# Where the operands of a seven-product round are split, in a one-core decoder step in float32

## The chip, the cores and the metric

The kernel runs on one core of a Trainium2 chip. It has a matrix engine (PE), three elementwise engines (DVE, the VectorE; ACT, the ScalarE; POOL, the GpSimd) and a queue (SP) from which nearly all DMA transfers of this kernel are issued, in the order in which they stand in the program. The metric is the time of one execution in microseconds. The kernel before takes 2215.38 us as the median of three runs (2211.3 to 2217.26).

## The reference

One layer of a decoder for 1024 prompt tokens and 8 single-token requests, width 1024, all in float32. The tokens are put side by side, T = 1032 columns. What matters here are the two feed-forward steps around the mixer:

```
def swiglu(x, w_up, w_down):
    gate, up = jnp.split(x @ w_up, 2, axis=-1)
    return (jax.nn.silu(gate) * up) @ w_down

hp = layer_norm(ALPHA * hp + 0.5 * swiglu(hp, ffn1_w_up[l], ffn1_w_down[l]), ln1_g[l], ln1_b[l])
...                                   # attention and retention, merged
hp = layer_norm(ALPHA * hp + 0.5 * swiglu(hp, ffn2_w_up[l], ffn2_w_down[l]), ln3_g[l], ln3_b[l])
```

The hidden width is 2816, 22 tiles of 128 features. The mixer between the two steps isn't touched by the change.

## The kernel before, in words

**Numbers in two parts.** A float32 operand is held as a high part, rounded to the matrix engine's fast type fp32r, and a low part, the rest. A product takes three matmuls: high by high, high by low, low by high. To split means: ACT copies x into the high part, and then another engine computes x minus the high part. Weight halves (128x512) are split so as they arrive: `w_hi` on ACT, `w_lo` on DVE.

**Seven products for eight.** Most of the two feed-forward steps is computed by a Strassen-Winograd form of 2x2 blocks. The weights of such a block are a quad of four halves and sums of them (`st`, made by DVE); the other operands are sums of token halves of 516 columns. One product is a unit of 24 matmuls of 258 columns. In the up-projection (units P, seven of them per feature tile, and C for the first tile) the operands are sums of the input. They lie in seven tiles TT[0] to TT[6], each 4T wide: 2T columns of high part, 2T of low part. `t_stage(i)` (L806) makes operand i from the residual tiles `ya` and `yb`: for a sum, two subtractions on DVE, then two ACT copies and two DVE subtractions for the two parts.

**The hidden values.** When a feature tile is done, `hidden` (L1435) gets it as `m`, two token halves. The first two and the last four tiles are stored plainly (`adr`). The sixteen between go in pairs: a is the even tile of a pair, b the odd one. From a pair the seven operands of the down-projection are made and stored to DRAM (`tdr`) as float32 numbers in one part: operand 0 is the first half of a, operand 1 the first half of b, 5 the second half of b, and 2, 3, 4 and 6 are differences (four DVE subtractions of 128x516, into the tiles `s`). There are two rounds (quads) of four pairs in each of the two feed-forward steps, so four rounds in all.

**The down-projection.** Its products are the units S: i = 0 to 6, for n = 0 to 3 in each round. The operands come back into the same seven tiles. As soon as a tile has had its last product (`rested`), `fetch_after` (L944) lets go the read of the next operand into it, at least 2 us of planned PE time after the read before. `fetch_one` (L929) reads 1032 KB from `tdr` into the low part's place, and `split` (L913) then makes the parts in two pieces of 128x1032: ACT copies, and DVE subtracts for operands 0, 2, 4 and 6, POOL for 1, 3 and 5. There are two lanes: the splits of one lane go one after the other, those of DVE and POOL side by side. A round of the down-projection begins with eight short units `dn` of 12 matmuls, which take a plain feature pair (two reads of 516 KB, split in pieces of 128x516, always on DVE). So a round is read while the units before it run: the last seven P units, or the last seven S units of the round before (n = 3), and the eight dn units behind them.

**The order of the work.** The kernel is written out by a planner in Python. It keeps a clock of PE (`E.pe`) and of each engine, a DMA queue (`E.dma` adds a transfer at 0.38 MB per us and 2 us for landing), and emits the side work when its due time comes. Each engine runs its instructions in the order in which they were emitted, whatever the true times are. `split` sleeps until the planned landing plus 1.5 us, and puts a piece on DVE only while DVE's planned backlog is at most 1.3 us (SHORT). `features` (L965) is called ahead of each S unit and finishes by force what its operand still lacks. PE's results are taken out of PSUM by ACT and DVE (`evac`); a PSUM bank is used again one or two units later, so a late evacuation stops PE.

**The tiles of the first step.** In the first feed-forward step the tiles 0 to 3 come from one pool and 4 to 6 from another; the down-projection used them in the order 1, 4, 5, 2, 3, 6, 0 (`qslot`), so its operands were read in the order 0, 3, 4, 1, 2, 5, in which the P units let the tiles go. In the second step the order is 1 to 6, 0.

**The start of the second up-projection.** Its units go C0, C1, P0, P1, C2, C3, P3, P2, then product 0 of the next feature tile, then P4, P5, P6. `before` (L1617) calls `t_stage(4)` ahead of P3 and `t_stage(6)` ahead of P2. The results of P3, P2 and of the next tile's product 0 are taken out by ACT copies.

Of the kernel before, what the change touches and what calls it, by code (L numbers as in the profile page):

```python
# [18 lines left out]
P = 128  # L19
# [17 lines left out]
QUADS = [(1, 2), (3, 4)]  # L37
QJ = [(2, 3, 0, 1), (0, 1, 2, 3)]
ORDER = [0, 1] + [GROUPS[g][k] for q in QUADS for k in range(4) for g in q] + GROUPS[5]
PLAIN = GROUPS[0] + GROUPS[5]  # L40
LAT = 0.2
HT = T // 2
# [6 lines left out]
NWARM = 3  # L49
START = 6.0  # L50
FETCH = 2.0
SHORT = 1.3
POOLD = (1, 4, 6)
AHEAD = 0.5
# [172 lines left out]
def build(tc, I, O):  # L227
# [3 lines left out]
    with ctx:  # L231
# [39 lines left out]
        scs = dram.tile([32, P], F32, name="scs")  # L271
        scv = dram.tile([1, 8, P], F32, name="scv")
        adr = [[dram.tile([P, T], F32, name=f"adr{p}_{i}") for i in range(len(PLAIN))] for p in range(2)]
        tdr = [[[dram.tile([P, 4, HT], F32, name=f"tdr{p}_{q}_{i}") for i in range(7)] for q in range(2)] for p in range(2)]
        hres = dram.tile([P, 4, T], F32, name="hres")
        dq = nc.gpsimd.dma_start
        ds = nc.sync.dma_start
# [24 lines left out]
                sbanks.put(b, E.pe)  # L302

        ta = ctx_open("ta", R)
        TT = [ta.tile([P, 4 * T], F32R, name=f"T{i}") for i in range(4)] + [None] * 3
        env["h"] = TT[:4]
        env["yb"] = ctx_open("y47", L).tile([P, 4, T], F32, name="yb")

        def open_y():
# [7 lines left out]

        def open_tb():
            p = ctx_open("tb", R)
            for i in range(4, 7):  # L320
                TT[i] = p.tile([P, 4 * T], F32R, name=f"T{i}")

        def open_sa():
            p = ctx_open("sw", R)
# [571 lines left out]

        qslot = [[[1, 4, 5, 2, 3, 6, 0], [4, 5, 2, 3, 6, 0, 1]], [[1, 2, 3, 4, 5, 6, 0], [2, 3, 4, 5, 6, 0, 1]]]
        fetches, fstate, rested, splits, lane = [], dict(t=0.0), {}, {}, [None, None]  # L900

        def fill(p):

            s0, s1 = qslot[p]
            res = [(0, ("U", 0), 0, k) for k in range(2)]
            res += [(s, ("U", s), "Q0", s0.index(s)) for s in range(1, 7)]
            res.append((0, "dn0", "Q0", 6))
            res += [(s0[0], (0, 0), 1, k) for k in range(2)]
            res += [(s0[i], (0, i), "Q1", i - 1) for i in range(1, 7)]
            res.append((s0[0], "dn1", "Q1", 6))  # L910
            return res + [(s1[i], (1, i), 5, 2 * i + k) for i in range(2) for k in range(2)]

        def split(hi, lo, n, t, pool):  # L913

            last, lane[pool] = lane[pool], None
            me = lane[pool] = [False]
            yield t
            while last is not None and not last[0]:
                yield E.pe + 0.2
            g = n // 2  # L920
            for k in (0, g):
                while not pool and E.eng["dve"] > E.pe + SHORT:
                    yield E.pe + 0.2
                t = E.act(hi[:, k:k + g], f(lo)[:, k:k + g], n=g)
                yield t
                (E.ptt if pool else E.tt)(lo[:, k:k + g], f(lo)[:, k:k + g], f(hi)[:, k:k + g], ALU.subtract, n=g)
            me[0] = True

        def fetch_one():  # L929
            p, i, _, g, k = fetches.pop(0)  # L930
            x = TT[i]
            if g in (0, 1, 5):
                o = k % 2 * 2 * T
                hi, lo = x[:, o:o + T], x[:, o + T:o + 2 * T]
                ds(out=f(lo), in_=adr[p][k + (2 if g == 5 else 0)])
                n = T
            else:
                hi, lo = x[:, 0:2 * T], x[:, 2 * T:4 * T]
                ds(out=f(lo), in_=tdr[p][int(g[1])][k].rearrange("p k n -> p (k n)"))
                n = 2 * T  # L940
            fstate["t"] = E.pe
            splits.setdefault((i, g), []).append(E.spawn(split(hi, lo, n, E.dma(n * 0.000512) + 1.5, n > T and k % 2)))

        def fetch_after(u):  # L944

            p = u["p"]
            if u["kind"] == "P":
                if u["ft"] != NF - 1:
                    return
                if u["i"] == 0:  # L950
                    fetches.extend((p,) + x for x in fill(p))
                    rested.clear()
                    splits.clear()
                rested["U", u["i"]] = True
            elif u["kind"] == "S" and u["n"] == 3:
                rested[u["q"], u["i"]] = True
            elif u["kind"] == "dn" and u["n"] == 7:
                rested[f"dn{u['part']}"] = True
            while fetches and fetches[0][2] in rested and (E.pe > fstate["t"] + FETCH or fetches[0][4] % 2 and fetches[0][3] in (0, 1, 5)):
                fetch_one()  # L960

        def dn_slot(u):
            return qslot[u["p"]][0][0] if u["part"] else 0

        def features(p, i, g):  # L965

# [468 lines left out]
        def hidden(p, ft, t):  # L1435
# [6 lines left out]
            q, k = (ft - 2) // 8, (ft - 2) % 8 // 2  # L1442
            s = env["s"]

            def out(i, src):
                ds(out=tdr[p][q][i][:, k, :], in_=src)
                E.dma(0.264)

            def sub(i, o, x, y):
                t = E.tt(o, x, y, ALU.subtract, n=HT)  # L1450
                E.later(t, lambda: out(i, o))

            if ft % 2 == 0:
                E.later(t, lambda: out(0, a[0]))
                E.later(t, lambda: sub(3, s[0], a[1], a[0]))
            else:
                E.later(t, lambda: out(1, b[0]))
                E.later(t, lambda: out(5, b[1]))
                E.later(t, lambda: sub(2, s[2], b[1], s[0]))
                E.later(t + 0.7, lambda: sub(4, s[1], b[1], a[1]))  # L1460
                E.later(t + 1.4, lambda: sub(6, s[3], b[0], s[2]))

        def evac_s(j, i, bank):

# [152 lines left out]
        def before(ui, u):  # L1617
            kind, c = u["kind"], u["c"]
            if kind == "P":
                p, ft, i = u["p"], u["ft"], u["i"]  # L1620
                if ft == 1:
# [13 lines left out]
                        stages([], [1] if p else [1, 2, 3])  # L1635
                    elif i == 3:
                        stages([4], [2, 3, 4, 5]) if p else stages([6], [6, 7])
                    elif i == 2 and p:
                        stages([6], [])
                    elif i == 4:  # L1640
                        end_t(p)
                        if p:
                            need(o + 6)
                        env["busy"] = False
# [46 lines left out]
                    start_d(u["p"])  # L1691
                features(u["p"], dn_slot(u), u["part"])
            if kind == "S":
                features(u["p"], qslot[u["p"]][u["q"]][u["i"]], f"Q{u['q']}")
            x = units[ui + 1] if ui + 1 < len(units) else u
            if x["kind"] == "S" and kind == "S" and x["q"] == u["q"]:
                features(u["p"], qslot[u["p"]][x["q"]][x["i"]], f"Q{x['q']}")
            if kind == "down":
                if u["first"]:
                    end_quads(u["p"])  # L1700
                for i in range(2):
                    features(u["p"], qslot[u["p"]][1][i], 5)
            if kind == "k":
                if c == 0:
                    ctx_close("tb")
# [9 lines left out]
        def operands(u):  # L1715
            kind, c = u["kind"], u["c"]
            n0, N = CH[c]
            if kind == "down":
                ks = []
                for i in range(4):  # L1720
                    x = TT[qslot[u["p"]][1][i // 2]]
                    o = i % 2 * 2 * T + n0
                    ks.append((u["dd"] * 4 + i, x[:, o:o + N], x[:, o + T:o + T + N]))
            elif kind in ("ao", "ro"):
# [13 lines left out]
        def product(u, bank):  # L1738

            if u["kind"] in ("P", "S"):  # L1740
                xs = [TT[u["i"] if u["kind"] == "P" else qslot[u["p"]][u["q"]][u["i"]]]]
# [222 lines left out]
```

## Time and profile before

| | |
|---|---|
| runs | 2211.3, 2215.38, 2217.26 us |
| the profiled execution's own time | 2217.32 us |
| its span, first to last instruction | 2215.5 us |
| mean granted PE clock | 0.987 |
| PE busy | 2133.7 us (96%), 15865 matmuls |
| DVE busy | 1495.8 us (68%) |
| ACT busy | 832.6 us (38%) |
| POOL busy | 268.5 us (12%) |
| DMA moved | 233.93 MB |

All times in the trace are us from the span's start. A row of a group gives the line, the engine, the operation, out<-in by tile names, partitions x elements, the count, the busy time, the mean in ns, and then the engine's idle time before these instructions with what ended it. All elementwise instructions are issued by a few helpers, so most have the same line (L119 for DVE, L115 for ACT, L135 for POOL), and the tile names tell them apart: `T<-T` is the split of a down-projection operand that was read from DRAM, `T<-ya` a split in `t_stage`, `yb<-pr` or `ya<-pr` an evacuation.

### The profile page before, as it was taken

What the parts mean: (1) busy time and instruction counts of PE and PEld (TensorE: products, weight loads), DVE (VectorE), ACT (ScalarE), POOL (GpSimd) and SP (SyncE); (2) the same over time, 40 slices, a digit from 0 to 9 for tenths busy, and PEclk for the clock granted to TensorE, in tenths of its full rate; (3) what the DMA queues carried; (4) which work ended last, traced back from release to release, by engine and by line L of the source; (5) the groups of instructions that cost most, each with busy time, mean ns of one, the idle gap of its engine ahead of it and who ended that gap; (6) DMA issues with size and microseconds to landing.
All of it is one profiled execution on the core that took longest, in us unless ns stands there. A gap on an engine that the chain in (4) does not pass through costs nothing.

```text
span 2215.5 us, 39506 instructions
## 1 busy us (share of the span) xinstructions
PE 2133.7 (96%) x15865; PEld 2096.7 (95%) x15865; DVE 1495.8 (68%) x2659; ACT 832.6 (38%) x1569; POOL 268.5 (12%) x259
## 2 busy tenths in 40 slices
PE   8999999999899999999999999998999999999996
PEld 7999999999899889999979999988999999999996
DVE  7666666685856885566676757777666666686757
ACT  5333333342423674111324434553333333433223
POOL 1000000020304333111110202010000000021103
PEclk9999999999999999999999999998999999999998
DMA  4322322261430110111263434531332232444222
GB/s 139 108 89 99 107 95 87 96 252 64 187 120 29 57 51 26 43 40 40 76 194 132 139 124 134 186 116 48 101 101 101 96 106 92 159 167 173 77 96 77
DMA packets 111705, 233.93 MB, mean 106 GB/s; under 512 B 13730, under 2 KB 17666, under 8 KB 107666
## 3 DMA queue, kind: packets, MB, share of 16 engines
q1 hardware_dynamic: 111170, 231.36, 30.9%
q8 instruction: 125, 2.05, 0.4%
q14 instruction: 58, 0.48, 0.1%
q0 software_dynamic: 352, 0.05, 0.0%
HBM read 186.56 MB, written 45.84 MB: 105 GB/s over the span
## 4 chain that ended last, share of the span: by engine, by line
PE 81%; DVE 10%; DMA 3%; issue 2%; ACT 2%; POOL 1%; SPq 0%; DVEq 0%; POOLq 0%; ACTq 0%
PE pr L97 54%; PE mb L97 25%; DVE T L119 2%; DMA raw<-in_w_dram 2%; DVE w_lo L119 2%; DVE ya L119 2%; PE sb L97 1%; DVE yb L119 1%; DVE ln L119 1%; DVE zt L119 1%; PE sb L105 1%; ACT w_hi L115 1%; ACT T L115 0%; POOL pt L135 0%; POOL ln L135 0%
## 5 line engine op out<-in xcount | busy, mean ns | idle before, releaser
L97 PE MATMUL pr<-T,w_hi 128*128 128x258 f32 x7008 | 1145.6, 286 | 45.9 <-DVE ya L119 14.6
L97 PEld LDWEIGHTS pr<-T,w_hi 128*128 128x128 f32 x7008 | 978.3, 192 | 53.0 <-DVE ya L119 14.0
L97 PE MATMUL pr<-T,w_lo 128*128 128x258 f32 x3504 | 713.2, 285 | 0.4 <-DVE w_lo L119 0.4
L97 PEld LDWEIGHTS pr<-T,w_lo 128*128 128x128 f32 x3504 | 551.4, 192 | 0.6 <-DVE w_lo L119 0.6
L97 PE MATMUL mb<-T,w_hi 128*128 128x384 f32 (+1 forms) x2208 | 526.2, 325 | 1.8 <-DVE yb L119 1.8
L119 DVE TENSOR_TENSOR w_lo<-raw,w_hi 128x512 fp32r<-128x512 f32 x500 | 360.0, 738 | 142.3 <-ACT w_hi L115 139.5
L115 ACT ACTIVATE w_hi<-raw 128x512 fp32r<-128x512 f32 x500 | 305.2, 625 | 290.3 <-PE pr L97 186.3
L97 PEld LDWEIGHTS mb<-T,w_hi 128*128 128x128 f32 x2208 | 378.0, 189 | 8.5 <-issue 5.0
L97 PE MATMUL mb<-T,w_lo 128*128 128x384 f32 (+1 forms) x1104 | 353.6, 320 | 0.0
L97 PEld LDWEIGHTS mb<-T,w_lo 128*128 128x128 f32 x1104 | 207.8, 188 | 0.0
L135 POOL TENSOR_TENSOR T<-T 128x1032 fp32r<-128x1032 f32 x24 | 67.1, 2813 | 1010.5 <-ACT T L115 1008.8
L115 ACT ACTIVATE w_hi<-st 128x512 fp32r<-128x512 f32 x174 | 108.4, 630 | 184.8 <-DVE st L119 98.4
L119 DVE TENSOR_TENSOR w_lo<-st,w_hi 128x512 fp32r<-128x512 f32 x174 | 123.1, 726 | 5.7 <-ACT w_hi L115 5.7
L119 DVE TENSOR_TENSOR a<-pr,a 128x516 f32<-128x516 f32 x87 | 60.5, 695 | 98.1 <-PE pr L97 94.4
L115 ACT ACTIVATE a<-pr 128x516 f32<-128x516 f32 x86 | 51.7, 601 | 132.7 <-PE pr L97 132.7
L119 DVE SCALAR_TENSOR_TENSOR ya<-pr,ya 128x516 f32<-128x516 f32 x72 | 49.4, 691 | 56.5 <-PE pr L97 56.3
L119 DVE SCALAR_TENSOR_TENSOR yb<-pr,yb 128x516 f32<-128x516 f32 x72 | 49.3, 691 | 55.5 <-PE pr L97 55.5
L119 DVE TENSOR_TENSOR T<-T 128x516 fp32r<-128x516 f32 (+1 forms) x64 | 86.7, 1354 | 0.0
L115 ACT ACTIVATE T<-T 128x1032 fp32r<-128x1032 f32 (+1 forms) x88 | 74.3, 895 | 15.1 <-DMA T<-tdr 14.4
L115 ACT ACTIVATE th<-a 128x516 f32<-128x516 f32 x43 | 27.3, 635 | 124.3 <-DVE a L119 124.3
L119 DVE TENSOR_TENSOR ln<-pr,ln 128x516 f32<-128x516 f32 x43 | 29.9, 695 | 53.5 <-PE pr L97 53.5
L119 DVE SCALAR_TENSOR_TENSOR gt<-gt,mb 128x384 f32<-128x384 f32 (+1 forms) x48 | 24.4, 509 | 59.8 <-PE mb L97 58.2
(316 smaller groups left out, 2230.2 us busy)
## 6 DMA issues: line engine op xcount, KB each, us to landing
raw<-in_w_dram SPq DMA_DIRECT2D x500, 256.0 KB, 3.0
T<-tdr SPq DMA_DIRECT2D x28, 1032.0 KB, 6.1
tdr<-ya SPq DMA_DIRECT2D x56, 258.0 KB, 3.1
tdr<-s SPq DMA_DIRECT2D x32, 258.0 KB, 2.7
T<-adr SPq DMA_DIRECT2D x16, 516.0 KB, 4.7
tdr<-m SPq DMA_DIRECT2D x24, 258.0 KB, 3.2
out_yp_dram<-zt SPq DMA_DIRECT2D x16, 256.0 KB, 2.0
adr<-m SPq DMA_DIRECT2D x5, 516.0 KB, 4.5
```

Source lines behind the costliest of these rows:

```text
L97: self.nc.tensor.matmul(out=out, lhsT=lhsT, rhs=rhs, start=start, stop=stop, **kw)
L105: self.nc.tensor.transpose(out=out, in_=in_, identity=ident)
L115: self.nc.scalar.activation(out=out, in_=in_, func=func, scale=scale, **kw)
L119: getattr(self.nc.vector, fn)(**kw)
L135: self.nc.gpsimd.tensor_tensor(out=out, in0=a, in1=b, op=op)
```

## The change

- `hidden` now stores operands 0 and 1 in two parts. For operand 0, ACT copies the first half of a into `s[1]` (high part), which is stored, and DVE subtracts it in place from a, which is stored as the low part; the same for b, into a's place. So each pair has six DVE subtractions of 128x516, two ACT copies and nine stores of 258 KB, where it had four, none and seven. Their order in time is written anew: two groups per pair (`first`; `second` and `third`).
- A read of operand 0 or 1 is 2064 KB and has no split behind it. The five other operands of a round are split as before, all on DVE, in one lane. POOL has no part in it.
- A read is let go only while the planned DMA queue is less than 8 us ahead of PE, besides the 2 us since the last read. A split wakes 0.7 us after the planned landing, not 1.5 us.
- In the first step the tiles are renamed, so that one order, 1 to 6 and 0, holds for both steps. The down-projection uses the same memory in the same order as before; the operands are now read in the order 0 to 5 there too.
- At the start of the second up-projection `t_stage(6)` moves from ahead of P2 to ahead of P4, past the units P2 and product 0 of the next tile and their ACT copies.

```diff
+WHOLE = (0, 1)
+QUEUE = 8.0
-        tdr = [[[dram.tile([P, 4, HT], F32, name=f"tdr{p}_{q}_{i}") for i in range(7)] for q in range(2)] for p in range(2)]
+        tdr = [[[dram.tile([P, 2 if i in WHOLE else 1, 4, HT], F32, name=f"tdr{p}_{q}_{i}") for i in range(7)] for q in range(2)]
+               for p in range(2)]
...
-        TT = [ta.tile([P, 4 * T], F32R, name=f"T{i}") for i in range(4)] + [None] * 3
-        env["h"] = TT[:4]
+        env["h"] = [ta.tile([P, 4 * T], F32R, name=f"T{i}") for i in range(4)]
+        TT = env["h"][:2] + [None] * 2 + env["h"][2:] + [None]
...
-        qslot = [[[1, 4, 5, 2, 3, 6, 0], [4, 5, 2, 3, 6, 0, 1]], [[1, 2, 3, 4, 5, 6, 0], [2, 3, 4, 5, 6, 0, 1]]]
+        qslot = [[1, 2, 3, 4, 5, 6, 0], [2, 3, 4, 5, 6, 0, 1]]
...
-        def split(hi, lo, n, t, pool):
+        def split(hi, lo, n, t):
-            last, lane[pool] = lane[pool], None
-            me = lane[pool] = [False]
+            last, me = lane[0], [False]
+            lane[0] = me
...
-                while not pool and E.eng["dve"] > E.pe + SHORT:
+                while E.eng["dve"] > E.pe + SHORT:
                     yield E.pe + 0.2
                 t = E.act(hi[:, k:k + g], f(lo)[:, k:k + g], n=g)
                 yield t
-                (E.ptt if pool else E.tt)(lo[:, k:k + g], f(lo)[:, k:k + g], f(hi)[:, k:k + g], ALU.subtract, n=g)
+                E.tt(lo[:, k:k + g], f(lo)[:, k:k + g], f(hi)[:, k:k + g], ALU.subtract, n=g)
...
-                ds(out=f(lo), in_=tdr[p][int(g[1])][k].rearrange("p k n -> p (k n)"))
                 n = 2 * T
+                src = tdr[p][int(g[1])][k].rearrange("p h k n -> p (h k n)")
+                fstate["t"] = E.pe
+                if k in WHOLE:
+                    ds(out=f(x), in_=src)
+                    E.dma(2.113)
+                    return
+                ds(out=f(lo), in_=src)
             fstate["t"] = E.pe
-            splits.setdefault((i, g), []).append(E.spawn(split(hi, lo, n, E.dma(n * 0.000512) + 1.5, n > T and k % 2)))
+            splits.setdefault((i, g), []).append(E.spawn(split(hi, lo, n, E.dma(n * 0.000512) + 0.7)))
...
-            while fetches and fetches[0][2] in rested and (E.pe > fstate["t"] + FETCH or fetches[0][4] % 2 and fetches[0][3] in (0, 1, 5)):
+            while fetches and fetches[0][2] in rested and (E.pe > fstate["t"] + FETCH and E.queue < E.pe + QUEUE or fetches[0][4] % 2 and fetches[0][3] in (0, 1, 5)):
...
-            def out(i, src):
-                ds(out=tdr[p][q][i][:, k, :], in_=src)
+            def out(i, src, lo=0):
+                ds(out=tdr[p][q][i][:, lo, k, :], in_=src)
                 E.dma(0.264)
-            def sub(i, o, x, y):
+            def sub(o, x, y, i=None, lo=0):
                 t = E.tt(o, x, y, ALU.subtract, n=HT)
+                if i is not None:
+                    E.later(t, lambda: out(i, o, lo))
+                return t
+            def high(o, x, i, t):
+                t = E.act(o.bitcast(F32R), x, n=HT, after=t)
                 E.later(t, lambda: out(i, o))
+                return t
+            def first():
+                sub(s[0], a[1], a[0], 3)
+                E.later(high(s[1], a[0], 0, t), lambda: sub(a[0], a[0], s[1], 0, 1))
-            if ft % 2 == 0:
-                E.later(t, lambda: out(0, a[0]))
-                E.later(t, lambda: sub(3, s[0], a[1], a[0]))
-            else:
-                E.later(t, lambda: out(1, b[0]))
+            def second():
                 E.later(t, lambda: out(5, b[1]))
-                E.later(t, lambda: sub(2, s[2], b[1], s[0]))
-                E.later(t + 0.7, lambda: sub(4, s[1], b[1], a[1]))
-                E.later(t + 1.4, lambda: sub(6, s[3], b[0], s[2]))
+                sub(s[2], b[1], s[0], 2)
+                sub(s[1], b[1], a[1], 4)
+                E.later(high(a[0], b[0], 1, t), third)
+            def third():
+                sub(s[3], b[0], s[2], 6)
+                sub(b[0], b[0], a[0], 1, 1)
+            E.later(t, second if ft % 2 else first)
...
-                    elif i == 2 and p:
-                        stages([6], [])
                     elif i == 4:
+                        stages([6] if p else [], [])
                         end_t(p)
```

More of the change, by code (lines that the diff above doesn't have):

```diff
@@ L319, in open_tb @@
             p = ctx_open("tb", R)
-            for i in range(4, 7):
-                TT[i] = p.tile([P, 4 * T], F32R, name=f"T{i}")
+            for i in (2, 3, 6):
+                TT[i] = p.tile([P, 4 * T], F32R, name=f"T{i + 2}")
         def open_sa():
@@ L895, in end_quads @@
                 ctx_close("sw")
-        qslot = [[[1, 4, 5, 2, 3, 6, 0], [4, 5, 2, 3, 6, 0, 1]], [[1, 2, 3, 4, 5, 6, 0], [2, 3, 4, 5, 6, 0, 1]]]
-        fetches, fstate, rested, splits, lane = [], dict(t=0.0), {}, {}, [None, None]
+        qslot = [[1, 2, 3, 4, 5, 6, 0], [2, 3, 4, 5, 6, 0, 1]]
+        fetches, fstate, rested, splits, lane = [], dict(t=0.0), {}, {}, [None]
         def fill(p):
-            s0, s1 = qslot[p]
+            s0, s1 = qslot
             res = [(0, ("U", 0), 0, k) for k in range(2)]
@@ L958, in fetch_after @@
                 rested[f"dn{u['part']}"] = True
-            while fetches and fetches[0][2] in rested and (E.pe > fstate["t"] + FETCH or fetches[0][4] % 2 and fetches[0][3] in (0, 1, 5)):
+            while fetches and fetches[0][2] in rested and (E.pe > fstate["t"] + FETCH and E.queue < E.pe + QUEUE or fetches[0][4] % 2 and fetches[0][3] in (0, 1, 5)):
                 fetch_one()
         def dn_slot(u):
-            return qslot[u["p"]][0][0] if u["part"] else 0
+            return qslot[0][0] if u["part"] else 0
         def features(p, i, g):
@@ L1693, in before @@
             if kind == "S":
-                features(u["p"], qslot[u["p"]][u["q"]][u["i"]], f"Q{u['q']}")
+                features(u["p"], qslot[u["q"]][u["i"]], f"Q{u['q']}")
             x = units[ui + 1] if ui + 1 < len(units) else u
             if x["kind"] == "S" and kind == "S" and x["q"] == u["q"]:
-                features(u["p"], qslot[u["p"]][x["q"]][x["i"]], f"Q{x['q']}")
+                features(u["p"], qslot[x["q"]][x["i"]], f"Q{x['q']}")
             if kind == "down":
@@ L1701, in before @@
                 for i in range(2):
-                    features(u["p"], qslot[u["p"]][1][i], 5)
+                    features(u["p"], qslot[1][i], 5)
             if kind == "k":
@@ L1720, in operands @@
                 for i in range(4):
-                    x = TT[qslot[u["p"]][1][i // 2]]
+                    x = TT[qslot[1][i // 2]]
                     o = i % 2 * 2 * T + n0
@@ L1740, in product @@
             if u["kind"] in ("P", "S"):
-                xs = [TT[u["i"] if u["kind"] == "P" else qslot[u["p"]][u["q"]][u["i"]]]]
+                xs = [TT[u["i"] if u["kind"] == "P" else qslot[u["q"]][u["i"]]]]
                 fresh = u["i"] in (0, 1, 3)
```

## The prediction

> **What bounds the kernel now.** First the page's busy times, to see which engine sets the end.
>
> ```profile
> span 2215.5 us, 39506 instructions
> PE 2133.7 (96%) x15865; PEld 2096.7 (95%) x15865; DVE 1495.8 (68%) x2659; ACT 832.6 (38%) x1569; POOL 268.5 (12%) x259
> ```
>
> PE is busy 96% of the span, and the change leaves its matmuls as they are. So only the time in which PE idles or runs at a lower clock can be won. Second, busy time by stretches: two long stretches of up-projection, and then the four stretches in which a round's operands are read and split. Columns: length, then busy us of PE, PE's weight load, DVE, ACT, POOL (instructions in brackets), granted clock, DMA share, GB/s.
>
> ```profile
> 100.00:440.00 340.00, 340.00 (x2814) 340.00 (x2813) 214.96 (x334) 118.26 (x201) 0.00 (x0) 1.00 0.28 98
> 1560.00:1925.00 365.00, 365.00 (x3028) 365.00 (x3028) 229.16 (x357) 127.22 (x218) 0.00 (x0) 1.00 0.29 98
> 445.00:500.00 55.00, 50.12 (x399) 49.59 (x398) 47.06 (x55) 27.85 (x39) 16.15 (x6) 0.97 0.69 255
> 553.00:600.00 47.00, 41.05 (x316) 40.63 (x315) 41.29 (x46) 21.44 (x28) 16.97 (x6) 0.93 0.56 210
> 1925.00:1970.00 45.00, 40.19 (x310) 39.47 (x308) 40.33 (x45) 22.66 (x33) 16.56 (x6) 0.92 0.77 283
> 2035.00:2075.00 40.00, 33.25 (x259) 32.66 (x258) 37.77 (x41) 20.16 (x25) 17.42 (x6) 0.96 0.50 176
> ```
>
> In the two long stretches PE has no idle time, POOL has nothing to do, and a matmul takes 340/2814 = 365/3028 = 0.1207 us. At that pace the matmuls of the four rounds would take 48.2, 38.1, 37.4 and 31.3 us. So the rounds lose 6.8 + 8.9 + 7.6 + 8.7 = **32.0 us**. Of these, length minus busy gives 4.9 + 5.9 + 4.8 + 6.8 = 22.4 us of idle PE; the other 9.6 us is a lower clock.
>
> Third, what the idle PE waited for. From the timeline of the third round, by engine: start, length, instruction, and in brackets the idle time before it.
>
> ```profile
> 1941.96 2.56 POOL L135 TENSOR_TENSOR T<-T 128x1032 fp32r<-128x1032 f32 x1 [1.41 <-ACT T L115]
> 1945.60 5.73 POOL L135 TENSOR_TENSOR T<-T 128x1032 fp32r<-128x1032 f32 x2 [1.08 <-ACT T L115]
> ...
> 1942.17 2.90 DVE L119 TENSOR_TENSOR w_lo<-raw,w_hi 128x512 fp32r<-128x512 f32 x1
> 1946.20 2.87 DVE L119 TENSOR_TENSOR w_lo<-st,w_hi 128x512 fp32r<-128x512 f32 x1
> 1949.00 0.68 DVE L119 SCALAR_TENSOR_TENSOR yb<-pr,yb 128x516 f32<-128x516 f32 x1
> 1949.60 2.81 DVE L119 TENSOR_TENSOR T<-T 128x1032 fp32r<-128x1032 f32 x1
> 1962.78 1.22 DVE L119 TENSOR_TENSOR T<-T 128x1032 fp32r<-128x1032 f32 x1
> ...
> 1945.73 0.75 PE L97 MATMUL pr<-T,w_hi 128*128 128x258 f32 x4 [1.00 <-DVE ya L119]
> 1949.73 0.75 PE L97 MATMUL pr<-T,w_hi 128*128 128x258 f32 x4 [2.27 <-DVE yb L119]
> 1953.08 1.23 PE L97 MATMUL pr<-T,w_hi 128*128 128x258 f32 x4 [1.54 <-DVE yb L119]
> ```
>
> While a POOL subtraction runs, a DVE subtraction that reads two SBUF tiles stands still until POOL is through: 1942.17 + 2.90 = 1945.07, against POOL's 1941.96 + 2.56 = 1944.52, after which DVE needs its own 0.6. A `w_lo` takes 2.9 us, and a split piece 2.81 us, where it takes 1.22 with POOL quiet (1962.78). The evacuation that reads PSUM isn't stretched (0.68 us at 1949.00, under POOL's 5.73), but it stands in DVE's order behind one that is, and PE waits for it. That is the stall of the rounds: not too much work on DVE, but work on DVE that waits for POOL.
>
> **The change part by part.** *POOL goes.* The groups by shape (count, busy us, mean ns, idle before them):
>
> ```profile
> L119 DVE TENSOR_TENSOR T<-T 128x1032 fp32r<-128x1032 f32 x32 | 60.2, 1881 | 0.0
> L135 POOL TENSOR_TENSOR T<-T 128x1032 fp32r<-128x1032 f32 x24 | 67.1, 2813 | 1010.5 <-ACT T L115 1008.8
> L115 ACT ACTIVATE T<-T 128x1032 fp32r<-128x1032 f32 x56 | 55.7, 1052 | 14.4 <-DMA T<-tdr 14.4
> L115 ACT ACTIVATE T<-T 128x516 fp32r<-128x516 f32 x32 | 18.9, 621 | 0.8 <-DMA T<-adr 0.6
> L119 DVE TENSOR_TENSOR s<-m,s 128x516 f32<-128x516 f32 x16 | 11.1, 694 | 0.3
> ```
>
> Per round DVE has eight long pieces at 1.88 = 15.0 us now; afterwards five operands in two pieces at 1.22 = 12.2 us. So it takes over two of POOL's operands and still has 2.8 us less to do, and the waiting `w_lo` (2.90 and 2.87 for 0.68 each) give back 4.4 us more. Nothing else on POOL falls into the rounds (six instructions in each, all splits). If every stall of a round goes, that is 32.0 us; if none, 0.
>
> What stays of them? The five splits now go one after the other. A product unit is 24 matmuls, 2.9 us; a `dn` unit 1.45 us. The first operand to be split, number 2, goes into the tile that the fourth unit of the round lets go. Ahead of it on the queue are 2 x 516 + 2 x 2064 KB, its own 1032 KB behind them, 6.3 MB in all. The fastest stretch of the trace gives the rate:
>
> ```profile
> 1930.00:1935.00 5.00, 5.00 (x43) 5.00 (x43) 4.28 (x8) 3.40 (x6) 0.00 (x0) 1.00 1.01 422
> 1945.00:1950.00 5.00, 2.00 (x14) 1.78 (x15) 5.00 (x6) 4.34 (x5) 4.40 (x2) 1.00 0.78 203
> 1950.00:1955.00 5.00, 3.46 (x21) 3.17 (x21) 5.00 (x4) 3.08 (x4) 3.26 (x2) 0.62 0.67 226
> 1970.00:2035.00 65.00, 65.00 (x541) 65.00 (x540) 38.82 (x60) 17.33 (x27) 0.00 (x0) 1.00 0.31 104
> ```
>
> At 0.42 MB per us that is 15 us, and some 18 with landing (estimate). The last split is wanted 3 + 3 units, eight `dn` and six S units later: 17.4 + 11.6 + 17.4 = 46.4 us after the first tile is free. That leaves 28 us for five splits. In plain S units DVE is busy 38.82 of 65 us, 0.60; since lengths overlap (a piece of 0.68 us is followed after 0.61), its occupation is nearer 0.53. A free share of 0.47 holds 12.2 us of splits in 26 us. So it fits, barely. I take 1.5 us of stall left per round (between 0 and all 8), 6.0 us.
>
> The clock term goes with the stalls: in the rows above the clock falls to 0.62 behind gaps of 1.00, 2.27 and 1.54 us. The Trainium skill, page "TensorE: Matmul & The Clock Gate", section "HAM oscillation", puts the limit at idle gaps of more than about 3.4 us; by it this third round, whose gaps are all shorter, would lose idle time only, 4.8 instead of 7.6, and the sum would be 2.8 us smaller. Here the row decides, since the lower clock stands in it.
>
> *Operands 0 and 1 in two parts.* 16 pairs get two more DVE subtractions (0.694 by the last row of the groups) and two ACT copies (0.621): 32 x 0.694 = 22.2 us of DVE and 19.9 us of ACT, all in the up-projections. Cover: there PE is 100% busy, DVE at 214.96 of 340 goes to 66%, ACT from 35% to 38%. The copies wait only for finished data and stores of a unit before. Without cover, that is if each subtraction held up an evacuation for its whole length, 22 us; it can't gain. I take +1, nearer to 0, because today's four subtractions stand in the same place and cost PE nothing. The 32 more stores (8.3 MB) fall where the DMA share is 0.28.
>
> *Reads.* Per round 2 x 1032 KB more, 5.0 us of full DMA. PE doesn't wait for it in the sum: at 1930 to 1935 DMA is full while PE is busy 5.00 of 5.00. Letting go by the queue and the earlier wake cost nothing by themselves; they are in the rivals. In the first step the read order now is the order of use; also 0.
>
> *`t_stage(6)`.* Rows of that place, by engine:
>
> ```profile
> 1521.85 2.37 DVE L119 TENSOR_TENSOR ya<-yb,ya 128x1032 f32<-128x1032 f32 x2
> 1524.21 2.38 DVE L119 TENSOR_TENSOR T<-ya,T 128x1032 fp32r<-128x1032 f32 x2
> 1526.85 0.69 DVE L119 TENSOR_TENSOR w_lo<-st,w_hi 128x512 fp32r<-128x512 f32 x1 [0.27 <-ACT w_hi L115]
> ...
> 1523.12 2.21 ACT L115 ACTIVATE T<-ya 128x1032 fp32r<-128x1032 f32 x2 [1.96 <-DVE ya L119]
> 1525.23 0.58 ACT L115 ACTIVATE ln<-pr 128x516 f32<-128x516 f32 x1
> ...
> 1525.86 1.23 PE L97 MATMUL pr<-T,w_hi 128*128 128x258 f32 x4 [5.67 <-ACT ln L115]
> ...
> 1520.00:1535.00 15.00, 9.33 (x57) 9.14 (x56) 9.79 (x11) 5.82 (x9) 0.00 (x0) 0.77 0.08 25
> ```
>
> PE waits 5.67 us for the evacuation of P2 (1525.23), which stands on ACT behind `t_stage(6)`'s copies, which wait for its sums. With the copies behind the evacuations, P4 can start when `t_stage(4)` is through, at 1521.85. Next late: P5's weights, whose `w_lo` stays behind `t_stage(6)` on DVE, to about 1527.2. P4 ends at 1524.8, so PE stalls some 2 us there. Bounds: this stretch loses 15 - 57 x 0.1207 = 8.1 us in all, so 0 to 8; I take 3.0, the idle time saved (5.67 - 1.6 - 2) and a part of the clock.
>
> **Sum**, against the profiled execution's own 2217.3: - 32.0 + 6.0 + 1.0 - 3.0 = 2189.3. That execution lies 1.9 above the median of the runs, so **2188** on their scale.
>
> **The rivals.** *DVE's one lane is late.* If the free share is 0.40, as the busy time says, five splits need 30.5 us where there are 28, and the lag grows by what evacuations and weights lose: at 3.5 us more per round, 14 us, so 2202. For it: DVE 5.00 of 5.00 in two of the rows. Against it: that fullness contains the waits for POOL. It decides from an occupation above 0.56. The Trainium skill, page "Perfetto Trace Analysis", section "Optimizing Scalar/DVE Operations", names moving work from a saturated DVE to other engines as what may help, which speaks against this change; it adds that between DVE and GpSimd it might not, and with that the rows agree.
>
> *ACT takes POOL's place, and the change doesn't do what it says.* A copy that wakes 0.8 us earlier stands waiting for its read, and the next `w_hi` behind it. Now ACT waits 14.4 us for 28 reads; 20 reads give 10.3 + 20 x 0.8 = 26 us, and if PE pays it all, 2214. Against it: ACT is busy 22.66 of 45 us in the round, and takes no evacuations in `dn` and S units. It decides when the next `w_hi` is wanted within the wait.
>
> *Slower: weights behind long reads.* The place is the SP queue, where weight loads stand behind reads.
>
> ```profile
> raw<-in_w_dram SPq DMA_DIRECT2D x500, 256.0 KB, 3.0
> T<-tdr SPq DMA_DIRECT2D x28, 1032.0 KB, 6.1
> ```
>
> A weight load lands after 3.0 us now (median). It may find 8 us of planned queue and a 2064 KB read (5.0 us) ahead, 13 us in all. If the weights have no more lead than they use now, PE pays 10 us per round: 2188 + 40 = 2228. It makes the kernel slower than before once PE pays over 6.8 us per round. Against it: no PE wait in the rounds is on weights, and DMA is already full for stretches there.
>
> **How the numbers follow.** Forecast 0.64 (2178 to 2198); late lane 0.16 (2202); ACT 0.09 (2214); weights 0.11 (2228). The range runs from all losses won without new cost, 2215.4 - 32.0 - 8.1 = 2175, to 2210, which leaves out the last two, 0.20. A change under 0.3%, 6.6 us, can't be told from none here. Faster: 0.64 + 0.16 and a bit of the third, 0.81; same 0.09; slower 0.10.
>
> **What would show it.** Right: no `T<-T` on POOL, `w_lo` in the rounds back at 0.7 us, `T<-T` on DVE 40 times near 1.22, the four stretches with PE idle under 2 us and the clock at 1.00, the wait of 5.67 us gone. Wrong on the lane: PE waits in the rounds for DVE with `T<-T` ahead, DVE full without stretched rows. Wrong on ACT: its idle time ended by `T<-tdr` above 20 us. Wrong on weights: PE or ACT idle until `raw` lands. Wrong on the up-projection: PE idle in the two long stretches.

## The result, and the profile after

| | before | after |
|---|---|---|
| median of the runs | 2216.32 us (4 runs, 2211.3 to 2219.83) | 2185.66 us (4 runs, 2184.0 to 2186.94) |
| profiled execution, span | 2215.5 us | 2185.2 us |
| mean granted clock | 0.987 | 0.992 |

The ratio is 0.9863, with a 95% interval of 0.9841 to 0.9884: about 30 us faster. The page's busy times of the changed kernel:

```profile
PE 2124.8 (97%) x15865; PEld 2089.1 (96%) x15865; DVE 1486.8 (68%) x2699; ACT 836.4 (38%) x1585; POOL 201.3 (9%) x235
```

PE has the same 15865 matmuls. POOL has lost 67.2 us and 24 instructions, the 24 splits. DVE has 40 instructions more and yet 9.0 us less busy time, which is only possible because its instructions have become shorter. The groups by shape say which (count, busy us, mean ns, idle before them); first two rows of the kernel before, then the changed one:

```profile
L119 DVE TENSOR_TENSOR w_lo<-raw,w_hi 128x512 fp32r<-128x512 f32 x500 | 360.0, 738 | 142.3 <-ACT w_hi L115 139.5 <-PE mb L97 2.1
L119 DVE TENSOR_TENSOR w_lo<-st,w_hi 128x512 fp32r<-128x512 f32 x174 | 123.1, 726 | 5.7 <-ACT w_hi L115 5.7
```

```profile
L121 DVE TENSOR_TENSOR w_lo<-raw,w_hi 128x512 fp32r<-128x512 f32 x500 | 355.8, 730 | 128.8 <-ACT w_hi L117 127.9
L121 DVE TENSOR_TENSOR w_lo<-st,w_hi 128x512 fp32r<-128x512 f32 x174 | 115.4, 683 | 5.0 <-ACT w_hi L117 5.0
L121 DVE TENSOR_TENSOR T<-T 128x1032 fp32r<-128x1032 f32 x40 | 48.5, 1224 | 0.0
L117 ACT ACTIVATE T<-T 128x1032 fp32r<-128x1032 f32 x40 | 40.6, 1054 | 17.1 <-DMA T<-tdr 17.1
```

A split piece on DVE takes 1.224 us, not 1.881. The 174 `w_lo<-st` have a mean of 0.683 us, not 0.726, and the two weight groups together have given back 4.2 + 7.7 = 11.9 us.

Busy time by stretches, with the up-projections in the first two rows and the four rounds behind them (length; busy us of PE, weight load, DVE, ACT, POOL; granted clock; DMA share; GB/s):

```profile
100.00:440.00 340.00, 340.00 (x2818) 340.00 (x2817) 223.92 (x349) 128.31 (x218) 0.00 (x0) 1.00 0.32 110
1560.00:1925.00 365.00, 365.00 (x3028) 365.00 (x3027) 240.23 (x375) 138.27 (x235) 0.00 (x0) 1.00 0.35 124
440.00:560.00 120.00, 117.88 (x975) 117.49 (x974) 82.86 (x123) 41.34 (x63) 0.00 (x0) 1.00 0.54 209
560.00:655.00 95.00, 95.00 (x787) 94.86 (x786) 66.80 (x99) 33.09 (x49) 0.00 (x0) 1.00 0.41 150
1900.00:1960.00 60.00, 57.55 (x464) 57.37 (x463) 45.78 (x65) 25.59 (x38) 0.00 (x0) 0.97 0.71 275
1960.00:2040.00 80.00, 80.00 (x665) 80.00 (x664) 53.18 (x80) 23.51 (x35) 0.00 (x0) 1.00 0.48 182
```

By the prediction's measure, length minus matmuls at 0.1207 us, the rounds now lose 120 - 975 x 0.1207 = 2.3, then 0, then 60 - 464 x 0.1207 = 4.0, then 0 (the second and fourth fit their length to 0.3 us): 6.3 us, where it was 32.0. The up-projections still have not a moment of idle PE, at 0.1207 us per matmul.

**Where the 30.3 us of span came from**, read from the same PE instructions in both traces: first step's rounds 13.5 us, second step's rounds 12.3, the units around `t_stage(6)` 2.9. That is 28.7. The rest lies elsewhere: in this execution the start of the kernel was 2.2 us shorter, the long first up-projection 0.5 shorter, the mixer with the first units behind it 1.1 longer, and the tail as long as before.

**What is left in the rounds.** The PE timeline of the first and third round, all waits over 0.25 us (start, length, instruction, the wait before it):

```profile
494.19 0.73 PE L99 MATMUL pr<-T,w_hi 128*128 128x258 f32 x4 [1.41 <-DVE yb L121]
...
498.25 0.51 PE L99 MATMUL pr<-T,w_hi 128*128 128x258 f32 x2 [0.71 <-DVE T L121]
...
1952.38 0.98 PE L99 MATMUL pr<-T,w_hi 128*128 128x258 f32 x4 [2.45 <-DVE yb L121]
```

The wait of 2.45 us names an evacuation on DVE. It would be easy to say that DVE has too much to do; its own timeline says otherwise:

```profile
1944.78 1.22 DVE L121 TENSOR_TENSOR T<-T 128x1032 fp32r<-128x1032 f32 x1
1949.01 0.69 DVE L121 TENSOR_TENSOR st<-raw,raw 128x512 f32<-128x512 f32 x1 [3.00 <-DMA raw<-in_w_dram]
...
1951.55 0.69 DVE L121 SCALAR_TENSOR_TENSOR yb<-pr,yb 128x516 f32<-128x516 f32 x1
```

DVE stood idle for 3.00 us until weights had landed, because the sums `st` of the next quad were the next instruction in its order, and the evacuation PE wanted stood four instructions behind them. Why the weights were late stands on the SP queue:

```profile
1925.12 0.32 SPq L1449 DMA_DIRECT2D adr<-ya  x1
1938.32 0.32 SPq L890 DMA_DIRECT2D ya<-hres  x1
1938.73 0.38 SPq L949 DMA_DIRECT2D T<-tdr  x1
1939.20 34.03 SPq L470 DMA_DIRECT2D raw<-in_w_dram  x8
```

The store `adr<-ya`, the last plain feature tile, is issued at 1925.12. Behind it stands the load `ya<-hres` (`start_d`, 2064 KB), which overwrites the tile that the store reads, so SP can't issue it until the store is through. The store shares its transfer queue with the reads issued ahead of it: from 1906.39 to 1925.12 these are 2 x 516 + 2 x 2064 + 4 x 1032 + 4 x 256 KB, 10.6 MB, with the store 11.1 MB, which at some 0.42 MB per us is 26 us, to about 1932 (an estimate; the DMA share is 1.00 in the five microseconds to 1935 and 0.40 in the next five). The load goes out at 1938.32, after 13.2 us in which SP issued nothing. Its queue's waits in this stretch (who waits for what; us, times, longest) give most of it to the store:

```profile
SPq L890 <- DMA adr<-ya: 10.8, 1, 10.8
```

The last operand read and the next weights stand behind the load, and its 2064 KB are ahead of theirs, though they need nothing of it. The chain of waits of this stretch goes the same way:

```profile
1925.12 13.18 DMA adr<-ya
...
1939.20 9.71 DMA raw<-in_w_dram
...
1949.01 0.70 DVE st L121
...
1952.38 7.66 PE pr L99 x49
```

In the first round such a store and load (named `adr<-m` and `ya<-in_x_dram` there) are issued at 468.06 and 480.26, and SP waits 10.8 us for the store there too.

### The profile page after: what moved, and what is told of

It reads as the page before. It is cut to its first block, busy times and chain, and to the rows that moved or that the text cites. A ratio compares the mean times of both kernels' runs of the same rounds, so it can differ in the third digit from the quotient of the medians.

```text
span 2185.2 us, 39568 instructions
## 1 busy us (share of the span) xinstructions
PE 2124.8 (97%) x15865; PEld 2089.1 (96%) x15865; DVE 1486.8 (68%) x2699; ACT 836.4 (38%) x1585; POOL 201.3 (9%) x235
## 4 chain that ended last, share of the span: by engine, by line
PE 82%; DVE 9%; DMA 4%; ACT 2%; issue 2%; POOL 1%; SPq 0%; DVEq 0%; ACTq 0%; POOLq 0%
PE pr L99 54%; PE mb L99 26%; DMA raw<-in_w_dram 3%; PE sb L99 1%; DVE T L121 1%; DVE ya L121 1%; DVE yb L121 1%; DVE w_lo L121 1%; DVE ln L121 1%; DVE zt L121 1%; ACT w_hi L117 1%; DMA adr<-ya 1%; PE sb L107 1%; DVE st L121 0%; ACT T L117 0%
## 5 line engine op out<-in xcount | busy, mean ns | idle before, releaser
L121 DVE TENSOR_TENSOR w_lo<-st,w_hi 128x512 fp32r<-128x512 f32 x174 | 115.4, 683 | 5.0 <-ACT w_hi L117 5.0
L137 POOL TENSOR_TENSOR ln<-ya 128x384 f32<-128x384 f32 (+1 forms) x6 | 6.8, 1127 | 776.2 <-DVE ya L121 776.1
L121 DVE TENSOR_TENSOR T<-T 128x1032 fp32r<-128x1032 f32 (+1 forms) x72 | 70.5, 986 | 0.3 <-ACT T L117 0.3
L117 ACT ACTIVATE T<-T 128x1032 fp32r<-128x1032 f32 (+1 forms) x72 | 59.6, 863 | 18.2 <-DMA T<-tdr 17.1
```

The lines of the kernel that those rows point to most:

```text
L117: self.nc.scalar.activation(out=out, in_=in_, func=func, scale=scale, **kw)
L121: getattr(self.nc.vector, fn)(**kw)
L137: self.nc.gpsimd.tensor_tensor(out=out, in0=a, in1=b, op=op)
```

## The experiments

Two theories were at stake first: that POOL's subtractions made DVE stand still, and that DVE simply had too much work. Then, after the traces above, that the residual is the place of the load of `ya`. Round losses are worked out as above. All kernels of a set ran on one chip beside the kernel before, whose median was 2216.56 us in the first set, 2215.89 in the second and 2215.5 in the third.

**1. The kernel before with POOL's splits in DVE's lane**, nothing else of the change.

```diff
-E.spawn(split(hi, lo, n, E.dma(n * 0.000512) + 1.5, n > T and k % 2))
+E.spawn(split(hi, lo, n, E.dma(n * 0.000512) + 1.5, 0))
```

> The kernel before with one edit: every split of a down-projection operand is on DVE, in one lane, seven per round; nothing else of the change. Theory (DVE's subtractions stand still while POOL runs): the stretched w_lo rows of 2.9 us go, POOL has no T<-T, and of the 32.0 us that the four rounds lose about 20 come back, since DVE then has 14 pieces of 1.22 = 17.1 us per round where it had 15.0 us of stretched ones: about 2196 us. Rival (DVE simply has too much work in the rounds): two more us of DVE work per round make it no faster than before, 2216 us or above. Rival (it is the two-part storage that does it): 2216 us.

Measured: 2196.19 us, ratio 0.9912 (0.9896 to 0.9927). Its groups by shape, and its PE and DVE timelines in the third round:

```profile
L119 DVE TENSOR_TENSOR w_lo<-st,w_hi 128x512 fp32r<-128x512 f32 x174 | 115.6, 683 | 5.4 <-ACT w_hi L115 5.4
L119 DVE TENSOR_TENSOR T<-T 128x1032 fp32r<-128x1032 f32 x56 | 68.4, 1225 | 0.0
```

```profile
1952.05 0.51 PE L97 MATMUL pr<-T,w_hi 128*128 128x258 f32 x2 [2.88 <-DVE T L119]
...
1948.23 0.69 DVE L119 TENSOR_TENSOR st<-raw,raw 128x512 f32<-128x512 f32 x1 [2.92 <-DMA raw<-in_w_dram]
```

DVE takes over all 24 pieces, 68.4 us of splits where it had 60.2, and the kernel is 20 us faster. Not one split or `w_lo` in the rounds is stretched any more. So it was not the amount of work. The rounds lose 11.6 us. The largest wait left in the third is on a split (`DVE T`), but that split stands in DVE's order behind the sums `st`, before which DVE was idle for 2.92 us until weights had landed, as above. So this wait doesn't show by itself that seven operands are too many for one lane; the two rounds without a load of `ya` lose 1.5 and 1.0 us here.

**2. The changed kernel with operands 3 and 5 back on POOL**, in a lane of their own.

```diff
-                while E.eng["dve"] > E.pe + SHORT:
+                while not pool and E.eng["dve"] > E.pe + SHORT:
...
-                E.tt(lo[:, k:k + g], f(lo)[:, k:k + g], f(hi)[:, k:k + g], ALU.subtract, n=g)
+                (E.ptt if pool else E.tt)(lo[:, k:k + g], f(lo)[:, k:k + g], f(hi)[:, k:k + g], ALU.subtract, n=g)
```

> The changed kernel with operands 3 and 5 split on POOL again, in a lane of their own; operands 0 and 1 are still stored in two parts. DVE then has 6 pieces per round where the changed kernel has 10. Theory (POOL stops DVE): four POOL pieces per round, 2.8 us each, bring two thirds of the loss back, since it was six pieces: 2186 + 17 = about 2203 us, with w_lo rows of 2.9 us in the rounds and PE waiting behind them. Rival (too much DVE work): with 4.9 us of DVE work less per round it is as fast as the changed kernel or faster, 2186 us or below.

Measured: 2192.06 us, ratio 0.9894 (0.9879 to 0.991).

```profile
L137 POOL TENSOR_TENSOR T<-T 128x1032 fp32r<-128x1032 f32 x16 | 40.8, 2570 | 1030.5 <-ACT T L117 1030.5
L121 DVE TENSOR_TENSOR T<-T 128x1032 fp32r<-128x1032 f32 x24 | 35.6, 1489 | 0.1
```

The stretching is back (a split piece on DVE at 1.489 for 1.224 us) and the rounds lose 12.0 us, where the changed kernel loses 6.3, though DVE has 13 us less to split. The direction is the theory's; the size is about a third of what it gave. As whole times the two kernels can't be told apart (their intervals overlap, and the profiled execution, 2196.35 us, is the slowest of the four); the stretched rows tell them apart, and the second and fourth round, which lose 2.4 and 2.2 us where the changed kernel loses nothing. Sixteen pieces do less harm than twenty-four, and not in proportion; that fewer of them meet a DVE subtraction on which PE is waiting is a likely reason, not a shown one.

**3. The changed kernel with all seven operands stored in one part**, and so all split on DVE.

```diff
-WHOLE = (0, 1)
+WHOLE = ()
```

with `hidden` as it was before.

> The changed kernel without the two-part storage: all seven operands are stored in one part as before, read as 1032 KB and split on DVE in the one lane; up-projection stores and subtractions as in the kernel before. DVE gets 4.9 us more per round, DMA 5 us less. Theory that DVE's lane holds 26 us of free time per round against 12.2 needed, and barely fits: with 17.1 us needed the splits come late, 2 to 4 us per round, so 2194 to 2202 us. Theory that what is left of stall in the first and third round comes from weights behind the long reads on the queue: these stalls of 2.3 and 4.0 us go and nothing comes in their place, 2180 us.

Measured: 2195.45 us, ratio 0.9905 (0.9888 to 0.9921). Its PE timeline, the largest waits of the first and third round, and what DVE did ahead of the second of them:

```profile
494.04 0.80 PE L99 MATMUL pr<-T,w_hi 128*128 128x258 f32 x2 [3.08 <-DVE T L121]
...
1955.67 0.80 PE L99 MATMUL pr<-T,w_hi 128*128 128x258 f32 x2 [4.69 <-DVE T L121]
...
1951.86 0.69 DVE L121 TENSOR_TENSOR st<-raw,raw 128x512 f32<-128x512 f32 x1 [4.73 <-DMA raw<-in_w_dram]
...
1954.40 1.23 DVE L121 TENSOR_TENSOR T<-T 128x1032 fp32r<-128x1032 f32 x1
```

The rounds lose 5.5 + 1.3 + 7.5 + 0 + 1.7 = 16.0 us (the fourth round lies in the last two stretches), 16.0 - 6.3 = 9.7 us more than with five splits. It would be easy to say that PE now waits for the split and not for weights. But ahead of the split DVE was idle for 4.73 us until weights had landed (3.12 us in the first round), and the split stood behind the four sums of them: it is the mechanism above once more, with a split left over behind it. What seven splits cost without it can be read only in the two rounds that have no load of `ya`: 1.3 and 1.7 us, where five cost nothing. How much of the other 6.7 us the lane would cost by itself isn't shown; no run has seven splits and the load elsewhere.

**4. The changed kernel without the condition on the queue.**

```diff
-(E.pe > fstate["t"] + FETCH and E.queue < E.pe + QUEUE or ...)
+(E.pe > fstate["t"] + FETCH or ...)
```

> The changed kernel without the condition on the planned queue; reads are let go 2 us after the last one as in the kernel before. If weight loads behind reads are what is left in the rounds: the reads are let go earlier, the loads stand behind more of them, and 2 to 8 us are lost in all, 2188 to 2194 us. If the condition never holds a read back (by the plan the queue is 5 us ahead at most when a tile comes free): no difference, 2186 us.

Measured: 2189.05 us, ratio 0.9875 (0.986 to 0.989). The rounds lose 6 us, as in the changed kernel. The condition has no effect that can be told.

**5. The changed kernel with `t_stage(6)` back ahead of P2.**

> The changed kernel with t_stage(6) back ahead of P2, nothing else. By the prediction's step the move is worth 3.0 us: PE's wait of 5.7 us for the evacuation of P2 is back, the waits of 1.5, 1.0 and 0.6 us at P4 and P5 are gone, 2188.6 us. Rival (the place costs the same either way, since P5's weights are late behind the sums): 2186 us.

Measured: 2192.51 us, ratio 0.9888 (0.9865 to 0.9912); as whole times this can't be told from the changed kernel. In its place it can. PE timeline of this kernel, then of the changed one:

```profile
1513.68 1.23 PE L99 MATMUL pr<-T,w_hi 128*128 128x258 f32 x4 [5.67 <-ACT ln L117]
```

```profile
1506.57 0.75 PE L99 MATMUL pr<-T,w_hi 128*128 128x258 f32 x4 [1.50 <-ACT ln L117]
...
1510.77 0.75 PE L99 MATMUL pr<-T,w_hi 128*128 128x258 f32 x4 [1.03 <-ACT w_hi L117]
...
1512.13 0.65 PE L99 MATMUL pr<-T,w_lo 128*128 128x258 f32 x2 [0.61 <-DVE w_lo L121]
```

One wait of 5.67 us has become three of 1.50, 1.03 and 0.61. From the same wait ahead of this place to the same wait behind it the stretch takes 27.5 us here and 25.2 in the changed kernel: 2.3 us. The traces of experiments 4 and 9 have the same three waits there, but need only 23.7 us: the granted clock, read microsecond by microsecond, stays at 1.00 behind the last of them, where in this trace of the changed kernel it is 0.50 from 1513 to 1515. So the move is worth 2.3 or 3.8 us, by whether the clock falls.

**6. The changed kernel with splits that wake 1.5 us after the planned landing**, not 0.7.

> The changed kernel with splits woken 1.5 us after the planned landing, as before, not 0.7. Rival on ACT (an earlier wake makes ACT stand waiting, and PE pays): ACT's idle time ended by reads falls from 17 us to under 8, and 3 us or more are won, 2183 us. If PE doesn't pay for ACT's waits: the same wait falls and the time stays at 2186 us.

Measured: 2188.99 us, ratio 0.9877 (0.9854 to 0.9901). By its groups ACT waits 16.7 us for the reads, against 17.1: nothing changes, in the wait or in the time. It was expected to fall below 8. So the wake constant doesn't set these waits, and since PE loses nothing in two of the rounds in which they occur, they are covered.

**7. The changed kernel with the load of `ya` later**: no longer in `start_d`, but ahead of the S unit of the first round with n = 1 and i = 0, by when the store is long through.

```diff
-            ds(out=env["ya"], in_=hres if p else xd[:, 0:4, :])
-            E.dma(2.114)
...
+                if (u["q"], u["n"], u["i"]) == (0, 1, 0):
+                    ds(out=env["ya"], in_=hres if u["p"] else xd[:, 0:4, :])
+                    E.dma(2.114)
```

> The changed kernel with the load of the residual halves ya (2064 KB) issued 7 product units later, ahead of product 0 of the round's second group of S units, and not ahead of the first dn unit. In the first and third round the queue now stands behind that load, which waits for a store of the hidden values (13.2 us in the third round), and eight weight loads behind it land after 9.6 us. If this is what is left of stall: the 2.3 and 4.0 us go, 2180 us. Rival (what is left comes from the lane of splits): the stalls stay, 2186 us; or the load now stands ahead of other weights and PE waits there.

Measured: 2180.98 us, ratio 0.9841 (0.9817 to 0.9865). Its SP queue in the third round, what that queue waits for, DVE's first sum of the new weights, and the stretches around the first and third round:

```profile
1923.45 0.32 SPq L1447 DMA_DIRECT2D adr<-ya  x1
1933.77 0.32 SPq L947 DMA_DIRECT2D T<-tdr  x1
1935.68 18.66 SPq L470 DMA_DIRECT2D raw<-in_w_dram  x5
1954.44 0.39 SPq L1714 DMA_DIRECT2D ya<-hres  x1
```

```profile
SPq L947 <- PE pr L99: 11.5, 3, 8.4
```

```profile
1940.22 0.69 DVE L121 TENSOR_TENSOR st<-raw,raw 128x512 f32<-128x512 f32 x1
```

```profile
440.00:560.00 120.00, 120.00 (x995) 119.84 (x994) 84.25 (x125) 42.14 (x64) 0.00 (x0) 1.00 0.56 212
1895.00:1965.00 70.00, 70.00 (x579) 69.82 (x578) 54.31 (x79) 28.73 (x42) 0.00 (x0) 1.00 0.64 246
```

PE is busy every moment of both stretches, and no round has a PE wait over 0.25 us. Counted from the store's issue, DVE begins the sums after 16.8 us (1940.22 - 1923.45), where it was 23.9 (1949.01 - 1925.12), and has not waited for them. Of these 7.1 us the smaller part is the wait on the queue: the weights go out 12.2 us behind the store instead of 14.1, because the read ahead of them now waits up to 8.4 us for its tile (`SPq L947 <- PE`), which the wait for the store had covered. The larger part, some 5 us, is the load's 2064 KB, which at 0.42 MB per us take 5.0 us (an estimate) and are no longer ahead. Since DVE's lane is the same as in the changed kernel, the lane itself costs nothing: the 0.71 us on `DVE T` at 498.25 had followed the wait before it.

**8. The same, with P5's weights also made ready ahead of `t_stage(6)`.**

```diff
-                        stages([6] if p else [], [])
-                        end_t(p)
                         if p:
                             need(o + 6)
+                        stages([6] if p else [], [])
+                        end_t(p)
```

> As the kernel with the late load of ya, and besides the weights of P5 at the start of the second up-projection are split ahead of t_stage(6), not behind it. PE's waits of 1.0 us for w_hi and 0.6 us for w_lo there go, T6 comes 0.6 us later for P6, which has slack: 1.6 us less than the kernel with the late load alone, about 2178 us, and faster than the changed kernel by 7 us.

Measured: 2181.89 us, ratio 0.9846 (0.9825 to 0.9866): no gain. The waits of 1.03 and 0.61 us are gone, and a new one stands in their place, on the PE timeline:

```profile
1513.90 0.72 PE L99 MATMUL pr<-T,w_hi 128*128 128x258 f32 x4 [1.03 <-DVE ln L121]
```

In its place that is 0.6 us less of idle PE, too little to be seen in the whole time.

**9. The changed kernel and the one with the late load, side by side on a third chip.**

> The changed kernel as it is, beside the kernel with the late load of ya, to compare the two on one chip: 2186 us, with waits of PE in the first and third round of 2 us each behind weights that land late.

> The kernel with the late load of ya once more, beside the changed kernel on one chip. If the late weights are what was left in the rounds: 5 us less than the changed kernel, 2181 us, no PE wait in any round. If the first measurement of it was luck: the same time as the changed kernel within 2 us.

Measured: changed 2190.07 us (4 runs, 2188.14 to 2191.61; ratio to before 0.9883, 0.9865 to 0.9901), late load 2180.31 us (5 runs, 2177.97 to 2182.36; 0.9842, 0.9824 to 0.9859). The runs of the two don't overlap. Third round of the changed kernel, then of the one with the late load:

```profile
1895.00:1965.00 70.00, 66.97 (x542) 66.79 (x542) 51.27 (x74) 29.29 (x44) 0.00 (x0) 0.98 0.65 250
```

```profile
1895.00:1965.00 70.00, 70.00 (x579) 69.85 (x579) 54.40 (x78) 28.76 (x42) 0.00 (x0) 1.00 0.65 247
```

The medians are 9.8 us apart. The rounds of the profiled executions explain 2.6 + 4.6 = 7.1 of it (120 - 973 x 0.1207 in the first, 70 - 542 x 0.1207 in the third). The expected 5 was too small in part because the third round's loss varies: 4.0 us in one execution, 4.6 in this one. What the remaining 2.7 us is stays open, but it is within the scatter of stretches that the edit doesn't touch: between these two profiled executions, 13.5 us apart, the mixer differs by 5.0 us and the start of the second up-projection by 1.8.

**10. The changed kernel with work for POOL that only writes**: two fills of 128x1032 with zeros ahead of each split piece of operands 3 and 5, overwritten by the copy behind them. The fills are added work.

```diff
+                for _ in range(2 * odd):
+                    nc.gpsimd.memset(f(hi)[:, k:k + g], 0.0)
                 t = E.act(hi[:, k:k + g], f(lo)[:, k:k + g], n=g)
```

> The changed kernel with two POOL instructions added ahead of each split piece of operands 3 and 5, that fill the high part's place (128x1032) with zeros, which ACT then overwrites; POOL writes SBUF here and reads nothing. If a DVE subtraction stands still for any POOL instruction: w_lo or T<-T rows stretched beyond 1.5 us while POOL runs, 2 us or more of PE waits per round, 2192 us or more. If it stands still only for POOL instructions that read SBUF, as the split on POOL does: no DVE row is stretched, and the time stays within 4 us of 2186 us; ACT starts some pieces later.

Measured: 2191.49 us in a single run, beside 2190.07 for the changed kernel on this chip, whose runs reach 2191.61. That is more than 4 us from the 2186 of the expectation, but no more than the changed kernel itself is here; the time decides nothing, the rows do. The timelines of POOL and DVE at the third round:

```profile
1927.16 3.90 POOL L928 MEMSET T<- 128x1032 f32 x4 [1.89 <-PE pr L99]
...
1927.76 0.68 DVE L121 TENSOR_TENSOR w_lo<-raw,w_hi 128x512 fp32r<-128x512 f32 x1
...
1929.78 0.68 DVE L121 TENSOR_TENSOR w_lo<-st,w_hi 128x512 fp32r<-128x512 f32 x1
```

Two subtractions of two SBUF tiles lie wholly or nearly so under POOL's fills and take 0.68 us, as ever. In the four rounds of this trace some thirty DVE additions and subtractions of two SBUF tiles meet a fill; none takes over 0.70 us, and the 40 long splits have their mean of 1.224 us. POOL at work is not what stops DVE; POOL's subtraction, which reads two SBUF tiles, is. The Trainium skill, page "SBUF — State Buffer", section "🔬 SBUF: two separate sides", says the same: the port pair that DVE and GpSimd share is an exclusive lock, and a DVE instruction with two SBUF inputs meets it only against a GpSimd instruction that reads SBUF. The traces agree (2.90 us for 0.68 under POOL's subtraction, 0.68 under its fill).

## Why the prediction was right

The forecast was 2188 us (its sum gives 2189.3 - 1.9 = 2187.4), the changed kernel takes 2185.66. By its steps:

- **The cause: right.** DVE waited for POOL and was not overloaded. Experiment 1 shows it by itself: more splits on DVE, no stretched row, 20 us won.
- **The size of the gain in the rounds: right as a sum, wrong in its parts.** The prediction took 32.0 out and left 6.0, as 1.5 us in each round from a lane that barely fits. Measured are 6.3, but as 2.3, 0, 4.0 and 0, and none of it is the lane: with the load of `ya` moved, the same lane costs nothing (experiment 7). The two amounts agree by chance. The working of the lane itself, room for five splits, was right. That they fit only barely isn't borne out: with seven, the two rounds in which DVE doesn't wait for weights lose 1.3 and 1.7 us (experiment 3). One of its signs of being right was missed narrowly: PE was to idle under 2 us in each round's stretch, and idles 2.1 us in the first and 2.45 in the third.
- **"Reads ... PE doesn't wait for it": the step that failed.** Its row, DMA full while PE is busy, was read rightly and is seen again: DMA at 1.00 does PE no harm by itself. What it missed is that weights stand in the same order: behind a load that waits for a store in that queue, and behind that load's own bytes. The third rival had this mechanism, weights behind long reads. Its price was 10 us for each round; measured are 2.3 and 4.0 in the two rounds that have a load of `ya` behind a store, 0 in the others.
- **The clock: right.** It came back with the gaps. Where a gap is left, it falls again: behind 2.45 us the third round loses 4.0 us, of which 60 - 57.55 = 2.45 is idle time and the other 1.5 is a lower clock (the five microseconds from 1950 are granted 0.76; behind that row stand two single microseconds of the same trace):

```profile
1950.00:1955.00 5.00, 2.62 (x13) 2.65 (x14) 5.00 (x9) 4.10 (x6) 0.00 (x0) 0.76 0.35 108
...
1953.00:1954.00 1.00, 1.00 (x6) 1.00 (x6) 1.00 (x3) 1.00 (x2) 0.00 (x0) 0.50 0.85 258
1957.00:1958.00 1.00, 1.00 (x11) 1.00 (x10) 1.00 (x2) 0.49 (x1) 0.00 (x0) 1.00 0.00 0
```

  The 0.76 is a mean, as is the 0.62 in the prediction: microsecond by microsecond the clock is 1.00 up to 1952, 0.50 for some 3.4 us, and 1.00 again. A gap doesn't always bring that. In experiment 4 it follows a wait of 1.94 us (first round) and doesn't follow one of 1.74 (third), and in the first round of the changed kernel waits of 1.41 and 0.71 us leave the clock at 1.00.

  The limit of about 3.4 us, on the Trainium skill's page "TensorE: Matmul & The Clock Gate", section "HAM oscillation", doesn't hold here, as in the trace of before; the row decided rightly.
- **Two parts in the up-projection: +1 predicted, 0 measured.** DVE went to 223.92 of 340 us (66%, as predicted), ACT to 38%, and PE is busy 340.00 of 340.00.
- **`t_stage(6)`: 3.0 predicted, 2.3 to 3.8 measured** (experiment 5; 2.9 between the traces before and after). P5's late weights were named, at some 2 us; they are 1.03 + 0.61.
- **The late lane, as a rival: not so**, by experiment 7. **ACT in POOL's place: not so.** Its wait for reads was to rise to 26 us; it is 17.1, longer per read than before, and costs PE nothing. The wake, which was to be its cause, has no effect on it (experiment 6).

The sum against the sum: 28.0 us were predicted of the change in span (32.0 - 6.0 - 1.0 + 3.0), 28.7 are found in the places of the change.

## What to carry to other kernels

An instruction that takes four times its usual length, as `w_lo` did here, is most likely waiting, whatever the busy share of its engine says: look for what runs beside it, and take that away before taking work off the engine. When a wait names an engine, ask what that engine was idle for just before; here "DVE late" was a weight load, and that one was late by a long load ahead of it on an in-order queue, which nobody needed yet; in experiments 1 and 3 "DVE's split late" was in part the same. A load that isn't urgent, above all one that overwrites a tile just stored, belongs behind the transfers that are.

## What the runs showed of the hardware

- A store of 516 KB issued behind 10.6 MB of reads held up the load that overwrites its source: SP waited 10.8 us for it. The median landing of a 256 KB weight load in the same execution is 2.9 us. While this queue was full, PE ran on without a gap.
- Moving only where one 2064 KB load of each step is issued brought the best version of this study: 2180.98 and 2180.31 us in two sets, ratios 0.9841 and 0.9842 to the kernel before.
- POOL's fills of 128x1032 take 0.96 us and leave DVE alone; its subtractions of the same size take 2.57 to 2.81 us and stop the DVE subtractions of two SBUF tiles in the rows shown. Whether a subtraction with only one SBUF input on POOL would also do so wasn't tried.
- The granted clock, read in single microseconds, was 1.00 or 0.50 with a mixed value where it changed. One low stretch of some 3.4 us costs about 1.5 us of matmuls (4.0 us lost for 2.45 us idle in the third round), and it came behind PE waits shorter than itself, though not behind all of them.
